# Even mixer of a two-layer decoder trunk: gates and compressed keys ahead of the attention rounds, scores two rounds ahead, exponentials by group; last FFN block and final root rewritten

## The chip, the core and the metric

The kernel runs on one core of a Trainium2 chip. The core has five engines with an instruction queue each: PE (TensorE, matmuls, with a separate queue of weight loads, PEld), DVE (VectorE), ACT (ScalarE), POOL (GpSimd) and SP (SyncE, which here only issues DMAs). Every engine works through its queue in order and waits at semaphores for the others. The metric is device time in microseconds (us) of one execution; times in the profile are us from the start of the span.

## The reference

Two layers, 256 tokens, width 1024. Each layer is `x += 1/2 FFN(norm x); x += mixer(norm x); x += 1/2 FFN(norm x)`, and a last RMSNorm follows. The FFNs are SwiGLU with 2816 hidden columns. The second (odd) layer's mixer, pooling and a diagonal state-space layer, is not touched. The first (even) layer's mixer, which is, computes:

```python
z = h @ w_in                                  # u, v, q, kc, vc, ks, vs, kw, vw, gate logits
# A, gMLP: per head, chunks of 128 tokens
v = (gelu(v) - mean) * rsqrt(var + eps)       # over the 64 columns of a head
s = einsum('hts,bcshd->bcthd', w_s * causal, v) + b
out_a = gelu(u) * s
# B, attention: three branches share q
kc, vc = gelu(blocks(kc) @ w1) @ w2, gelu(blocks(vc) @ w1) @ w2   # compressed keys, 15 blocks
p_c = softmax(q kc * scale)                   # branch 1
o_s = softmax(q ks * scale, causal) @ vs      # branch 2 (all 4 blocks are selected at 256 tokens)
o_w = softmax(q kw * scale, causal) @ vw      # branch 3 (the window of 512 covers all)
out_b = sigmoid(gate) weighted sum of the three
m = concatenate([out_a, out_b]) @ w_out
```

The final norm is `x * rsqrt(mean(x*x) + 1e-6) * g`.

## The kernel before, in words

**Matmuls.** x is kept transposed in SBUF as eight tiles of 128 columns by 256 tokens (`x`, and its split into a high part `xh` and a low part `xl`). Every weight is split too, into `wh` (ACT, a cast, L98) and `wl` (DVE, a subtraction, L108), and each product is the sum of three matmuls: high·high, high·low, low·high (L123 to L125 for products by rows, L134 to L141 for projections, L164 to L166 where tokens are the rows). So the PE does three matmuls of 256 columns where one would stand.

**Weights.** They lie in one stream of units of 128x1024 values, two to a DMA (`raw`, three buffers, issued by SP). `unit` takes the split unit that is due, `used` counts it, and `split_to` then casts and subtracts the next one, up to six units ahead (seven buffers of `wh` and `wl`). With `at["hold"]` set, `used` splits nothing. With `at["wait"]` set, `split_to` casts at once but leaves the DVE subtraction in the list `lows`, from which `chain` takes one after each of two of its ACT steps (`lower(1)`) and `lower()` the rest.

**FFN** (`ffn`). 22 blocks of 128 hidden columns. Block j: two units of gate and up (`proj`, 48 matmuls), `chain(j)` (DVE `e`, ACT `s`, DVE `h`, ACT `hh`, DVE `hl`), then `down(j - 1)` (24 matmuls). After the last block `down(21)` comes directly behind `down(20)`. In all blocks from the fourth on `at["wait"]` is set during `proj`.

**Even mixer** (`even`). The order is written out by hand, since each engine's queue keeps program order. First the projections kk, q0, q1 and v (until 230.5 us in the profile), with rotary embedding on DVE, and `gv`, the gelu of v, on ACT. Then the narrow projection n (values and gate logits, tokens as rows, in banks 2 and 3). Then six rounds of attention: two for the first 128 tokens (four heads a group, width 128, one for each branch) and four for the second (two heads a group, width 256). A round has two groups g. For round i:

- `scores(i)`: PE, into banks 0 and 1, one a group, with the causal mask added by a bf16 matmul; DVE takes the maxima `am` (L555, L556); ACT takes exponentials with the row sums `alr` (L559)
- `norm(i, g)`: DVE multiplies by gate over row sum (L568 to L571)
- `turn(i, g)`: PE transposes four blocks into bank 3 (`pt`, L577), ACT copies them out (`pts`, L579)
- `mix(i)`: PE multiplies by the values `vn`, into banks 6 and 7 (`oT`, L588)

The generator `filling` gives dense matmuls to put between these: compressed keys cc, gate projections u0 and u1, and the first quarter of the output product (`half_out`). The work of branch A and of the compressed keys (`hps`, `kps`, `hid`, `cmp_scores`, `cmp_probs`, `cmp_pv`, `spatial`, `variance`) hangs between the steps of the filling. Round i's scores are written while round i-1 is under way. PSUM has eight banks and each is reused under several names; a name's first write waits for the last reader of the name before. `close` splits `oT` for the output product.

**End.** After the last FFN the sums of squares go through 28 matmuls to `ms` (L228), `rstd` computes the inverse root from an integer guess and three Newton steps on DVE (12 small instructions), 16 transposes turn x into `fo`, and four scaled copies `xo` (two on DVE, two on ACT) go out by four DMAs, two issued by SP and two by ACT.

Of the kernel before, what the change touches and what calls it, by code (L numbers as in the profile page):

```python
# [16 lines left out]
D = 1024  # L17
T = 256
# [18 lines left out]
def even_units():  # L37
    return (pair_units("kk", "q0") + pair_units("q1")
            + [("v", k) for k in range(4)] + [("n", k) for k in range(3)]
            + pair_units("cc") + pair_units("u0") + pair_units("u1")  # L40
            + [("eo", d, k) for d, k in ((0, 0), (0, 1), (1, 0), (1, 1), (0, 2), (1, 2), (0, 3), (1, 3))])
# [16 lines left out]
def trunk(ctx, tc, a, out):  # L58
# [121 lines left out]
    V.memset(ones, 1.0)  # L180
    zero = cst.tile([128, 512], BF, name="zero")
# [35 lines left out]
    def rsqrt(y, v, shape):  # L217
        t = wk.tile(shape, F32, tag=f"rs{shape[1]}", name="rs")
        V.tensor_scalar(y.bitcast(I32), v.bitcast(I32), 1, None, op0=OP.logical_shift_right)
        V.tensor_scalar(y.bitcast(I32), y.bitcast(I32), -1.0, float(0x5F3759DF), op0=OP.mult, op1=OP.add)  # L220
        for _ in range(3):
            V.tensor_tensor(t, y, y, op=OP.mult)
            V.scalar_tensor_tensor(t, t, -0.5, v, op0=OP.mult, op1=OP.mult)
            V.scalar_tensor_tensor(y, t, 1.5, y, op0=OP.add, op1=OP.mult)
# [31 lines left out]
    def ffn(f, after):  # L256
# [41 lines left out]
        for j in range(3, NM):  # L298
# [5 lines left out]
            at["wait"] = True  # L304
# [5 lines left out]
            used()  # L310
        down(NM - 1, after)
        used()

    def even(after):
# [66 lines left out]
        def steps(name, o, halves, done=None):  # L381
            for half in halves:
                for k in range(4):
                    pairs([(name, o)], half, (k,))
                    if k == 3:
                        if half and done:
                            done()
                        used()
                    yield

# [8 lines left out]
        def filling():  # L399
            cps = bank(4, "cps")  # L400
            yield from steps("cc", cps, (0, 1), lambda: widen(cps))
            hps = bank(2, "hps")
            ups = bank(5, "ups")
            for n, _ in enumerate(steps("u0", ups, (0, 1), lambda: ugate(0, ups))):
                for l in (2 * n, 2 * n + 1):
                    P.matmul(hps[:, 0:68], w1[:, l], zcv[:, :, l:l + 529:16], start=l == 0, stop=l == 15)
                if n == 7:
                    V.tensor_copy(hs[0:64], hps[64:128, 1:34])
                    V.tensor_copy(hs[64:128], hps[0:64, 34:67])
                    V.tensor_tensor(hs[0:64], hs[0:64], hps[0:64, 0:33], op=OP.add)  # L410
                    V.tensor_tensor(hs[64:128], hs[64:128], hps[64:128, 35:68], op=OP.add)
                    S.activation(hid[:, :, 0:15], hs[:, 0:32].rearrange("p (g n) -> p g n", g=2)[:, :, 0:15],
                                 AF.Gelu_apprx_tanh, bias=hs[:, 32:33])
                    S.activation(gu[:, 0:2], gu[:, 0:2], AF.Gelu_apprx_tanh)
                    G.tensor_copy(hr[64:128], hid[64:128, :, None, :].to_broadcast([64, 2, 4, 16]))
                yield
            ups1 = bank(5, "ups")
            u1 = steps("u1", ups1, (0, 1), lambda: ugate(1, ups1))

            def dense(g, n=1):  # L420
                for _ in range(n):
                    next(g)
                    yield

            yield from dense(u1, 3)
            kps = bank(2, "kps")
            for g in range(2):
                P.matmul(kps[64 * g:64 * g + 64, 16 * g:16 * g + 16], w2[0:64, :], hid[0:64, g], start=True,
                         stop=True, skip_group_check=True)
            vps2 = bank(4, "vps2")  # L430
            P.matmul(vps2[:, 0:64], hr[64:128].rearrange("p a b c -> p (a b c)"), w2[64:128, :], start=True,
                     stop=True, skip_group_check=True)
            for g in range(2):
                V.tensor_copy(kz[64 * g:64 * g + 64, 16 * g:16 * g + 16], kps[64 * g:64 * g + 64, 16 * g:16 * g + 16])
            V.tensor_tensor(kzs, kz, cse[:, 1], op=OP.mult)
            V.tensor_tensor(kz, kz, cse[:, 0], op=OP.mult)
            V.tensor_tensor(vc.rearrange("p a b c -> p (a b) c"), msel.rearrange("p a b c -> p (a b) c"),
                            vps2[:, None, 0:64].to_broadcast([128, 8, 64]), op=OP.mult)
            yield from dense(u1, 1)
            sp = [spatial(0, 4), spatial(1, 2)]  # L440
            next(sp[0])
            next(sp[0])
            yield
            yield from dense(u1, 1)
            kps = bank(2, "kps2")
            P.matmul(kps[:, 0:32], rot, kzs, start=True, stop=True, skip_group_check=True)
            V.tensor_tensor(kcr, kz, kps[:, 0:32], op=OP.add)
# [1027 lines left out]
```

## Time and profile before

| | |
|---|---|
| three timed runs | 989.79, 990.17 (median), 990.9 us |
| the profiled execution's own time | 990.87 us |
| its span | 989.2 us |
| PE busy | 959.7 us (97%) |
| DVE, ACT, POOL busy | 631.5 (64%), 485.4 (49%), 294.0 us (30%) |
| DMA | 175.47 MB, mean 177 GB/s |

Within the span, the FFN of the first layer runs to 201 us, its mixer to 331.7, the two FFNs that follow to about 717, the odd mixer to about 789, and the last FFN to 977.8. A busy PE is not a PE at full rate: matmul ends are modelled, so the steps from one matmul's start to the next's say more than the busy share. PEclk is the clock that the throttle granted, 1.00 at full rate.

### The profile page before, as it was taken

The page shows a single profiled execution, that of the slowest core. Times are in us where ns is not written, and L with a number is a line of the kernel's source. Part 1 is how long each engine was busy: PE and PEld are TensorE (multiplying, and loading weights), DVE is VectorE, ACT ScalarE, POOL GpSimd, SP SyncE. Part 2 cuts the span into 40 slices and gives each one's busy share as a digit, 9 for nine tenths or more (in the row PEclk, how much of TensorE's full clock was granted, in tenths as well). Part 3 has the DMA queues.
Part 4 walks back from the last instruction along what each step waited for, and adds up shares of the span by engine and source line. Part 5 has one row for each costly group of instructions (what it writes and reads, how often), then busy time and mean ns, then how long its engine had stood idle before and what let it go on. Part 6 is the DMA issues. An engine that isn't in the chain of part 4 may idle for free.

```text
span 989.2 us, 19297 instructions
## 1 busy us (share of the span) xinstructions
PE 959.7 (97%) x8075; PEld 936.7 (95%) x8075; DVE 631.5 (64%) x943; ACT 485.4 (49%) x741; POOL 294.0 (30%) x461
## 2 busy tenths in 40 slices
PE   8999999999878999999999999999999999999997
PEld 6999999998757999999999999999998999999997
DVE  6766655587755775555548754557778676555554
ACT  6544444477544554444445543444465555444442
POOL 1399979010020235554401531438010000000001
PEclk9999999999989999999999999999999999999998
DMA  7655655544312464545443645694553445445431
GB/s 258 244 208 200 227 214 185 207 135 164 129 43 85 164 225 179 197 181 190 180 170 129 233 182 183 208 260 156 211 164 124 180 170 199 187 173 211 171 129 43
DMA packets 32856, 175.47 MB, mean 177 GB/s; under 512 B 7792, under 2 KB 10032, under 8 KB 12928
## 3 DMA queue, kind: packets, MB, share of 16 engines
q1 hardware_dynamic: 29696, 166.21, 46.4%
q0 software_dynamic: 2496, 7.41, 2.8%
q8 instruction: 63, 1.03, 0.4%
q10 hardware_dynamic: 576, 0.62, 0.2%
q14 instruction: 25, 0.20, 0.1%
HBM read 172.12 MB, written 2.10 MB: 176 GB/s over the span
## 4 chain that ended last, share of the span: by engine, by line
PE 87%; DVE 6%; ACT 2%; issue 2%; DMA 1%; POOL 1%; SPq 1%; ACTq 0%; POOLq 0%; DVEq 0%
PE gu L134 16%; PE gu L136 16%; PE gu L141 16%; PE y L125 9%; PE y L124 9%; PE y L123 9%; DVE wl L108 2%; DMA raw<-in_ws 1%; ACT pr L559 1%; DVE pr L571 1%; PE ms L228 0%; PE sc L547 0%; PE glu L125 0%; PE zc L164 0%; PE zd L134 0%
## 5 line engine op out<-in xcount | busy, mean ns | idle before, releaser
L108 DVE TENSOR_TENSOR wl<-raw,wh 128x1024 fp32r<-128x1024 f32 x308 | 382.0, 1252 | 14.9 <-ACT wh L98 14.9
L134 PE MATMUL gu<-xh,wh 128*128 128x256 f32 x1408 | 365.2, 282 | 1.4 <-ACT wh L739 1.1
L136 PE MATMUL gu<-xh,wl 128*128 128x256 f32 x1408 | 364.0, 282 | 0.7 <-DVE wl L740 0.4
L98 ACT CAST wh<-raw 128x1024 fp32r<-128x1024 f32 x308 | 312.0, 1049 | 90.4 <-PE gu L141 41.5
L141 PE MATMUL gu<-xl,wh 128*128 128x256 f32 x1408 | 275.9, 281 | 0.0
L134 PEld LDWEIGHTS gu<-xh,wh 128*128 128x128 f32 x1408 | 265.7, 189 | 3.7 <-ACT wh L739 2.9
L136 PEld LDWEIGHTS gu<-xh,wl 128*128 128x128 f32 x1408 | 264.8, 188 | 2.1 <-DVE wl L740 1.8
L261 DVE TENSOR_TENSOR e<-gu,rb 128x512 f32<-128x512 f32 x88 | 60.8, 690 | 256.9 <-PE gu L141 255.7
L141 PEld LDWEIGHTS gu<-xl,wh 128*128 128x128 f32 x1408 | 213.7, 188 | 0.0
L125 PE MATMUL y<-hl,wh 128*128 128x256 f32 x704 | 198.6, 282 | 1.6 <-DVE hl L272 1.6
L123 PE MATMUL y<-hh,wh 128*128 128x256 f32 x704 | 198.2, 282 | 1.2 <-ACT hh L270 1.2
L124 PE MATMUL y<-hh,wl 128*128 128x256 f32 x704 | 198.3, 282 | 0.0
L264 ACT ACTIVATE s<-e 128x256 f32<-128x256 f32 x88 | 36.8, 418 | 204.4 <-DVE e L261 204.3
L125 PEld LDWEIGHTS y<-hl,wh 128*128 128x128 f32 x704 | 132.5, 188 | 2.4 <-DVE hl L272 2.4
L123 PEld LDWEIGHTS y<-hh,wh 128*128 128x128 f32 x704 | 132.6, 188 | 1.6 <-ACT hh L270 1.4
L124 PEld LDWEIGHTS y<-hh,wl 128*128 128x128 f32 x704 | 132.6, 188 | 0.0
L270 ACT CAST hh<-h 128x256 fp32r<-128x256 f32 x88 | 35.8, 407 | 85.5 <-DVE h L267 85.5
L300 POOL COPY pace<-hl 128x1 f32<-128x1 f32 x25 | 25.0, 1001 | 151.5 <-DVE hl L272 151.5
L206 POOL TENSOR_TENSOR sq<-sq 128x512 f32<-128x512 f32 x10 | 13.7, 1365 | 187.2 <-ACT sq L204 119.0
L761 POOL TENSOR_SCALAR sq<-x,gw 128x256 f32<-128x256 f32 x4 | 3.6, 918 | 184.2 <-DVE x L752 184.2
L789 POOL TENSOR_TENSOR sq<-sq 128x64 f32<-128x64 f32 (+1 forms) x120 | 53.3, 463 | 3.6
L267 DVE TENSOR_TENSOR h<-s,e 128x256 f32<-128x256 f32 x88 | 39.4, 448 | 8.2 <-ACT s L264 8.2
(334 smaller groups left out, 1138.5 us busy)
## 6 DMA issues: line engine op xcount, KB each, us to landing
raw<-in_ws SPq DMA_DIRECT2D x154, 1024.0 KB, 4.8
toep<-kd POOLq DMA_DIRECT2D x8, 256.0 KB, 9.7
raw<-in_ws SPq DMA_DIRECT2D x4, 256.0 KB, 4.4
raw<-in_ws SPq DMA_DIRECT2D x2, 512.0 KB, 8.2
w<-in_w POOLq DMA_DIRECT2D x1, 1024.0 KB, 5.1
bnd<-in_bnd POOLq DMA_DIRECT2D x1, 544.0 KB, 5.5
x<-in_x SPq DMA_DIRECT2D x4, 128.0 KB, 3.6
x<-in_x SPq DMA_DIRECT2D x2, 256.0 KB, 7.5
```

Source lines behind the costliest of these rows:

```text
L98: S.copy(h, src)
L108: V.tensor_tensor(lo, src, h.bitcast(F32), op=OP.subtract)
L123: P.matmul(o, h, ah, start=first, stop=False, skip_group_check=True)
L124: P.matmul(o, lo, ah, start=False, stop=False, skip_group_check=True)
L125: P.matmul(o, h, al, start=False, stop=last, skip_group_check=True)
L134: P.matmul(os, h[:, c], xh[:, 4 * half + k], start=half == 0 and k == 0 and s == 0, stop=False, skip_group_check=True)
L136: P.matmul(os, lo[:, c], xh[:, 4 * half + k], start=False, stop=False, skip_group_check=True)
L141: P.matmul(o[:, T * s:T * s + T], h[:, c], xl[:, 4 * half + k], start=False, stop=half == 1 and k == 3, skip_group_check=True)
L261: V.tensor_tensor(e, gu[j].rearrange("p (a b) -> p a b", a=2), rb[:, None, :].to_broadcast([128, 2, T]), op=OP.mult)
L264: S.activation(s, e[:, 0], AF.Silu)
L267: V.tensor_tensor(h, s, e[:, 1], op=OP.mult)
L789: steps.append(lambda: G.tensor_tensor(o, p, q, op=op))
```

## The change

In the even mixer:

- The weight stream has u0, cc and u1 before n, and the output units in another order.
- `filling` is taken apart. u0, cc and u1 are projected first, without attention between them (`ahead`). `variance` (now with its square on ACT) stands between the halves of cc; `spatial(0)` stands in front of u1's fourth step, the 16 compression matmuls `hps` between its last four.
- All four gelus come before the exponential table is loaded. Then `scores(0)` and its exponentials, then n in three pieces (`narrow`) with `spatial(1)`, `kps` and the rotation of the compressed keys between them. `ah` and `al` get tiles of their own, since n still reads `xh`.
- `scores(i)` no longer does the exponentials; `expo(i, g)` does, per group. Round i now goes: for each group the transposes of round i and, on ACT behind the copy of the transposes, the exponentials of round i+1, then DVE's `norm` of round i+1; after both groups `mix(i)` and `scores(i + 2)`.
- The filling in the rounds is output product alone: three units, 24 steps of three matmuls. One weight unit is split per round.

In `ffn` the last block no longer sets `at["wait"]`, so its two subtractions stand ahead of `chain(21)`. At the end the inverse root is ACT's square root (its table loaded before `down(21)`), a reciprocal and one Newton step, and all four output DMAs are issued by SP.

Three places in the order. The first is PE in u1, and what POOL has there. `sps` are the spatial matmuls, `gv` the normalized v. Before, they stood behind the second mix:

```order
L141 MATMUL ups<-xl,wh 128x256 x2
L588 MATMUL oT<-pts,vn 64x2x128 x4
L480 MATMUL sps<-wst,gv 128x128 x4
L134 MATMUL ups<-xh,wh 128x256
L136 MATMUL ups<-xh,wl 128x256
```

Now they stand in u1's projection, ahead of all attention:

```order
L141 MATMUL ups<-xl,wh 128x256 x2
L406 MATMUL sps<-wst,gv 128x128 x4
L134 MATMUL ups<-xh,wh 128x256
L136 MATMUL ups<-xh,wl 128x256
L134 MATMUL ups<-xh,wh 128x256
L136 MATMUL ups<-xh,wl 128x256
L141 MATMUL ups<-xl,wh 128x256 x2
L590 MATMUL hps<-zcv,w_130 128x68 x4
```

The spatial matmuls moved ahead of six rounds, the variance that they need with them, from inside the first round to cc. On ACT, the same stretch now reads, with one table load after the gelus:

```order
L365 ACT_TABLE_LOAD
L365 ACTIVATE gv<-v_2901,rc 128x8x64
L365 ACTIVATE gv<-v_2902,rc 128x8x64
L98 CAST wh<-raw 128x1024 x2
L575 ACTIVATE sq<-sq 128x512
L98 CAST wh<-raw 128x1024
L556 ACTIVATE sq<-gv 128x1024
L98 CAST wh<-raw 128x1024 x2
L600 ACTIVATE hid<-hs 128x2x15
L602 ACTIVATE sq<-sq 128x512
L604 ACT_TABLE_LOAD
L604 ACTIVATE gate<-ones 128x1
```

The square of gv (L556) now stands behind the gelu of u0 (L575) and a cast. The second place is where the rounds begin, on PE. Before, n was followed by the scores and dense cc:

```order
L166 MATMUL n_3011<-wh,xl 128x280
L547 MATMUL sc<-roped 128x128 x8
L550 LDWEIGHTS identb
L550 MATMUL sc<-negb,identb 128x512
L550 LDWEIGHTS identb
L550 MATMUL sc<-negb,identb 128x512
L134 MATMUL cps<-xh,wh 128x256
```

Now the scores of round 1 stand there, six dense matmuls, and the first transposes:

```order
L473 MATMUL sc<-roped 128x128 x8
L476 LDWEIGHTS identb
L476 MATMUL sc<-negb,identb 128x512
L476 LDWEIGHTS identb
L476 MATMUL sc<-negb,identb 128x512
L123 MATMUL y<-ah,wh 128x256
L124 MATMUL y<-ah,wl 128x256
L125 MATMUL y<-al,wh 128x256
L123 MATMUL y<-ah,wh 128x256
L124 MATMUL y<-ah,wl 128x256
L125 MATMUL y<-al,wh 128x256
L509 MATMUL pt<-ident,pr 128x128 x4
```

DVE has this between the gate's last step and the copy of the values out of bank 3, into which those transposes go:

```order
L643 TENSOR_SCALAR sg<-sg 128x48
L500 RECIPROCAL alr<-alr 128x4
L501 TENSOR_TENSOR alr<-alr,sg 128x4
L503 TENSOR_SCALAR pr<-pr,alr 128x128 x4
...
L480 TENSOR_REDUCE am<-sc 128x4
L481 TENSOR_SCALAR am<-am 128x4
...
L648 TENSOR_SCALAR vn<-n_3277,rc 128x256
L648 TENSOR_SCALAR vn<-n_3278,rc 128x256
```

The lines left out repeat the three of `norm` and the two of the maxima for the second group. The copies `vn`, which before came ahead of the gate and both norms, now come behind them and behind the maxima of round 1. The third place is the end of a first FFN on DVE, before and now:

```order
L261 TENSOR_TENSOR e<-gu,rb 128x512
L108 TENSOR_TENSOR wl<-raw,wh 128x1024
L267 TENSOR_TENSOR h<-s,e 128x256
L108 TENSOR_TENSOR wl<-raw,wh 128x1024
L272 TENSOR_TENSOR hl<-h,hh 128x256
```

```order
L108 TENSOR_TENSOR wl<-raw,wh 128x1024 x3
L266 TENSOR_TENSOR e<-gu,rb 128x512
L272 TENSOR_TENSOR h<-s,e 128x256
L277 TENSOR_TENSOR hl<-h,hh 128x256
```

The two subtractions between the steps of the chain now stand ahead of it. The diff, with the moved bodies cut:

```diff
     return (pair_units("kk", "q0") + pair_units("q1")
-            + [("v", k) for k in range(4)] + [("n", k) for k in range(3)]
-            + pair_units("cc") + pair_units("u0") + pair_units("u1")
+            + [("v", k) for k in range(4)] + pair_units("u0") + pair_units("cc") + pair_units("u1")
+            + [("n", k) for k in range(3)]
...
-            at["wait"] = True
+            at["wait"] = j < NM - 1
...
+        if f == 3:
+            S.activation(gate, ones[:, 0:1], AF.Sqrt)
         down(NM - 1, after)
...
+        ups = bank(5, "ups")
+        ahead("u0", ups)
+        ugate(0, ups)
+        S.activation(gu[:, 0:2], gu[:, 0:2], AF.Gelu_apprx_tanh)
+        cps = bank(7, "cps")
+        pairs([("cc", cps)], 0)
+        used()
+        variance()
+        pairs([("cc", cps)], 1)
+        widen(cps)
+        used()
...
+        def early(n):
+            if n == 3:
+                spatial(0, 5)
+            for l in range(4 * n - 16, 4 * n - 12) if n > 3 else ():
+                P.matmul(hps[:, 0:68], w1[:, l], zcv[:, :, l:l + 529:16], start=l == 0, stop=l == 15)
...
+        ahead("u1", ups1, early)
...
+        S.activation(gate, ones[:, 0:1], AF.Exp)
+        spatial_out(0)
+        scores(0)
+        expo(0, 0)
+        expo(0, 1)
...
+        narrow(2)
+        P.matmul(kps[:, 128:160], rot, kzs, start=True, stop=True, skip_group_check=True)
         for t in range(2):
-            V.tensor_scalar(vn[:, t], nps[t][:, 0:256], rc[:, t:t + 1], None, op0=OP.mult)
             S.activation(sg[:, t], nps[t][:, 256:280], AF.Tanh, scale=hrc[:, t:t + 1])
...
         for g in range(2):
             norm(0, g)
+        scores(1)
+        for t in range(2):
+            V.tensor_scalar(vn[:, t], nps[t][:, 0:256], rc[:, t:t + 1], None, op0=OP.mult)
...
+        go(2)
+        for i in range(6):
+            for g in range(2):
+                turn(i, g)
+                if i < 5:
+                    expo(i + 1, g)
+                    norm(i + 1, g)
+                go(1 if g and i in (2, 3) else 2)
+            if i == 1:
+                cmp_probs()
+            elif i == 2:
+                cmp_transpose()
+            mix(i)
+            if i < 4:
+                scores(i + 2)
+            if i == 0:
+                cmp_scores()
+            elif i == 3:
+                for b in range(2):
+                    cmp_pv(b)
+                close(0)
+            split_to(min(at["used"] + AHEAD, at["split"] + 1))
...
-    rstd(ms)
+    root = wk.tile([128, 2], F32, tag="msv", name="root")
+    S.activation(root, ms[:, 0:2], AF.Sqrt, scale=1.0 / D, bias=eps)
+    mean = wk.tile([128, 2], F32, tag="rs2", name="mean")
+    V.tensor_scalar(mean, ms[:, 0:2], 1.0 / D, 1e-6, op0=OP.mult, op1=OP.add)
+    V.reciprocal(rc, root)
+    newton(rc, mean, wk.tile([128, 2], F32, tag="rs2", name="rs"))
...
-            (nc.scalar if t else nc.sync).dma_start(out[128 * t:128 * t + 128, 512 * h2:512 * h2 + 512], o)
+            nc.sync.dma_start(out[128 * t:128 * t + 128, 512 * h2:512 * h2 + 512], o)
```

More of the change, by code (lines that the diff above doesn't have):

```diff
@@ L379, in even @@
         vc = gm.tile([128, 4, 2, 64], F32, name="vc")
[L381 to L389, printed above, removed]
         def ugate(i, o):
@@ L397, in widen @@
                 V.tensor_tensor(v2(zcv[r, i, 0:512]), v2(o)[r], rb[r, None, :].to_broadcast([64, 2, T]), op=OP.mult)
[L399 to L447, printed above, removed]
-            yield from dense(u1, 1)
-            next(sp[0], None)
-            yield from dense(u1, 1)
-            next(sp[1])
-            yield
-            yield from dense(u1, 1)
-            S.activation(gu[:, 2:4], gu[:, 2:4], AF.Gelu_apprx_tanh)
-            next(sp[1])
-            y[0:2] = [bank(4, "y"), bank(5, "y")]
-            out0 = half_out(0, 0, True, False)
-            yield from dense(out0, 2)
-            next(sp[1], None)
-            yield from cmp_scores()
-            yield from dense(out0, 5)
-            cmp_probs()
-            yield from dense(out0, 1)
-            out1 = half_out(0, 1, False, False)
-            yield from dense(out1, 2)
-            cmp_transpose()
-            yield
-            for b in range(2):
-                cmp_pv(b)
-                yield
-            yield from dense(out1, 6)
@@ L473, in even @@
-        ah, al = xh[:, 0:4], xl[:, 0:4]
+        ah = gm.tile([128, 4, T], F32R, name="ah")
+        al = gm.tile([128, 4, T], F32R, name="al")
+        gated = {}
         def spatial(i, b):
@@ L507, in cmp_scores @@
                              stop=t == 1 and j == 3, skip_group_check=True)
-                if not t:
-                    yield
             V.tensor_tensor(pc, sc[:, 0:256].rearrange("p (t h n) -> p t h n", t=2, h=8),
@@ L629, in variance, with ahead, narrow @@
             G.memset(kz, 0.0)
-        fill = filling()
-        def go(n):
-            for _ in range(n):
-                next(fill, None)
+        def ahead(name, o, before=None):
+            for half in range(2):
+                for k in range(4):
+                    if before:
+                        before(4 * half + k)
+                    pairs([(name, o)], half, (k,))
+                used()
[9 more added lines that the diff above has]
+        widen(cps)
+        used()
+        hps = bank(4, "hps")
+        ups1 = bank(6, "ups")
+        def early(n):
[3 more added lines that the diff above has]
+                P.matmul(hps[:, 0:68], w1[:, l], zcv[:, :, l:l + 529:16], start=l == 0, stop=l == 15)
+            if n == 7:
+                at["hold"] = True
+        ahead("u1", ups1, early)
+        V.tensor_copy(hs[0:64], hps[64:128, 1:34])
+        V.tensor_copy(hs[64:128], hps[0:64, 34:67])
+        V.tensor_tensor(hs[0:64], hs[0:64], hps[0:64, 0:33], op=OP.add)
+        V.tensor_tensor(hs[64:128], hs[64:128], hps[64:128, 35:68], op=OP.add)
+        ugate(1, ups1)
+        S.activation(hid[:, :, 0:15], hs[:, 0:32].rearrange("p (g n) -> p g n", g=2)[:, :, 0:15],
+                     AF.Gelu_apprx_tanh, bias=hs[:, 32:33])
+        S.activation(gu[:, 2:4], gu[:, 2:4], AF.Gelu_apprx_tanh)
+        G.tensor_copy(hr[64:128], hid[64:128, :, None, :].to_broadcast([64, 2, 4, 16]))
+        S.activation(gate, ones[:, 0:1], AF.Exp)
[3 more added lines that the diff above has]
+        expo(0, 1)
+        V.tensor_scalar(hrc, rc, 0.5, None, op0=OP.mult)
         nps = [bank(2, "n0"), bank(3, "n1")]
-        at["hold"] = True
-        for n in range(3):
+        kps = bank(6, "kps")
+        def narrow(n):
             h, lo = unit(("n", n))
```

99 lines of the change are left out of this document (54 added, 45 removed).

## The prediction

> **What bounds the kernel now.** I read the page's busy shares first, then the waits of PE over the whole span, then the stretches of the even mixer by granted clock, then PE's timeline at the waits.
>
> ```profile
> PE 959.7 (97%) x8075; PEld 936.7 (95%) x8075; DVE 631.5 (64%) x943; ACT 485.4 (49%) x741; POOL 294.0 (30%) x461
> ```
>
> PE is busy nearly throughout, so a gain can only come from PE's idle time, from a low clock, or from the two ends. Who PE waits for (us in total, times, longest):
>
> ```profile
> PE pt L577 <- ACT pts L579: 8.3, 4, 3.8
> PE sps L480 <- DVE vc L437: 4.0, 1, 4.0
> PE pctp L529 <- POOL pc L524: 1.9, 1, 1.9
> PE y L125 <- DVE hl L272: 1.6, 3, 0.5
> ...
> PE kps L428 <- ACT hid L412: 1.3, 1, 1.3
> ...
> PE oT L534 <- ACT pct L530: 0.5, 1, 0.5
> ```
>
> All but the fourth row lie in the even mixer: 8.3 + 4.0 + 1.9 + 1.3 + 0.5 = 16.0 us of idle PE. The fourth is the end of three FFNs. Then the clock (PEclk) and three places of PE's timeline, where the bracket is the idle time before:
>
> ```profile
> 240.00:250.00 10.00, 7.18 (x53) 6.36 (x54) 8.13 (x21) 9.24 (x23) 0.00 (x0) 0.88 0.14 40
> 300.00:310.00 10.00, 7.68 (x55) 5.55 (x53) 4.98 (x14) 3.45 (x9) 1.47 (x1) 1.00 0.30 107
> ```
>
> ```profile
> 247.76 1.12 PE L577 MATMUL pt<-ident,pr 128*128 128x128 f32 x4 [2.74 <-ACT pts L579]
> 274.67 1.81 PE L480 MATMUL sps<-wst,gv 128*128 128x128 f32 x8 [3.95 <-DVE vc L437]
> 282.77 1.06 PE L480 MATMUL sps<-wst,gv 128*128 128x128 f32 x8
> 312.99 0.66 PE L577 MATMUL pt<-ident,pr 128*128 128x128 f32 x4 [1.06 <-ACT pts L579]
> ```
>
> After an idle time of 2.74 or 3.95 us the same work is slower: transposes 1.12 against 0.66 us, spatial matmuls 1.81 against 1.06. The 1.9 us wait for `pc` (it ends at 302.9) leaves the clock at 1.00. Three waits are long enough (2.74, 3.95 and the 3.8 of the first waits row). The slow time after one is about 3.5 us, in which half the work is done, so each costs some 1.7 us, 2.5 after the longest; I put the three at 5.8. So the mixer holds 16.0 + 5.8 = 21.8 us that a better order could at most win back. The question is how much of it returns as new waits.
>
> **The new PE order, first wait.** The stretch that changes runs between these two starts, and the row between them gives the length of a unit:
>
> ```profile
> 230.48 0.29 PE L164 MATMUL n<-wh,xh 128*128 128x280 f32 x1
> 317.43 0.39 PE L123 MATMUL y<-xh,wh 128*128 128x256 f32 x1
> 331.72 0.28 PE L134 MATMUL gu<-xh,wh 128*128 128x256 f32 x1
> ```
>
> From 317.43 to 331.72 PE does five units of 24 matmuls without a wait: 14.29 / 5 = 2.86 us a unit. From 230.48 it now does u0 (two units, 5.7), cc (5.7) and three of u1's eight steps (2.1), and at 244.0 it reaches the spatial matmuls. They need `gv`, centred and scaled. That chain crosses four engines:
>
> ```profile
> 233.13 0.18 DVE L362 TENSOR_SCALAR mu<-mu 128x16 f32<-128x16 f32 x1
> 245.17 1.11 ACT L659 ACTIVATE sq<-gv 128x1024 f32<-128x1024 f32 x1
> 255.99 1.22 DVE L624 TENSOR_REDUCE var<-sq 128x16 f32<-128x1024 f32 x1
> 259.86 1.91 POOL L627 TENSOR_TENSOR gv<-gv,rstd 128x1024 f32<-128x1024 f32 x1 [24.50 <-DVE alr L568]
> 263.50 0.68 DVE L392 TENSOR_TENSOR sq<-ups,rb 128x512 f32<-128x512 f32 x1
> 285.69 1.05 ACT L98 CAST wh<-raw 128x1024 fp32r<-128x1024 f32 x1
> 292.04 0.62 POOL L514 TENSOR_TENSOR pc<-pc,cm 128x256 f32<-128x256 f32 x1
> 301.16 1.22 DVE L108 TENSOR_TENSOR wl<-raw,wh 128x1024 fp32r<-128x1024 f32 x1
> 301.39 1.47 POOL L524 TENSOR_TENSOR pc<-pc,cl 128x256 f32<-128x256 f32 x1 [8.72 <-DVE cl L523]
> ```
>
> The last three rows show POOL and DVE excluding each other: a POOL product that takes 0.62 us alone took 1.47 when it came 0.23 us after a DVE subtraction of 1.22. So: `mu` is done at 233.3; DVE starts a `wl` (to 234.5); POOL's centring, which nothing hindered before, waits for it and takes 1.91 (to 236.4); DVE's next `wl` waits for that (to 237.6); then u0's scaling (238.3), on ACT its gelu (0.6), a cast (1.05) and the square (about 1.0, to 241.0); DVE, with a `wl` until 241.2, needs from the reduction's start to POOL's 259.86 - 255.99 = 3.9 us (245.0); POOL scales (1.91, to 246.9). PE waits 246.9 - 244.0 = **2.9 us**. Without the exclusion it is 1.3 less (wl, gelu and square start when u0 is done, at 236.2), and this is the lower end; a cast or two more in the way is the upper, 4.5. An idle time of 2.9 lies above the 2.74 that was followed by a low clock: plus 1.6.
>
> What is queued behind on PE is all of the mixer, so nothing covers this wait.
>
> **Second wait.** The first transposes of round 0 go into bank 3, which `vn` must have emptied. DVE does that behind the gate, two norms and the maxima of round 1.
>
> ```profile
> 236.74 1.16 PE L547 MATMUL sc<-roped 64*128 64x128 f32 x16
> 238.09 0.47 PE L134 MATMUL cps<-xh,wh 128*128 128x256 f32 x1
> 239.93 0.87 DVE L652 TENSOR_SCALAR vn<-n,rc 128x256 f32<-128x256 f32 x2
> 242.01 0.49 ACT L653 ACTIVATE sg<-n,hrc 128x24 f32<-128x24 f32 x2
> 245.04 4.62 DVE L108 TENSOR_TENSOR wl<-raw,wh 128x1024 fp32r<-128x1024 f32 x4
> 252.25 0.69 DVE L555 TENSOR_REDUCE am<-sc 128x4 f32<-128x512 f32 x1
> 253.77 0.17 DVE L556 TENSOR_SCALAR am<-am 128x4 f32<-128x4 f32 x1
> ```
>
> From the last matmul of n: the gate and both norms 245.04 - 242.01 = 3.0 us, the maxima 253.9 - 252.25 = 1.7, `vn` 0.9, hand-overs 0.1: 5.7. In that time PE has the rotation (0.3), the scores of round 1 (238.09 - 236.74 = 1.35) and six dense matmuls (0.7, with the change of shape 0.9): 2.55. PE waits **3.1 us**, and 1.7 for the clock. Bounds: 2.5 (maxima overlapped as well as possible, by 0.6) to 3.9 (POOL's last product of branch A, near 1.3 us, in the way of `sg`, by 0.8).
>
> **The rounds.** Four table loads of ACT (after the first gelu of a group and back) leave the mixer's middle, and with them the waits that they feed. ACT's work in a round of the second half is now:
>
> ```profile
> 281.63 0.59 ACT L579 COPY pts<-pt 128x512 f32<-128x512 f32 x1 [0.80 <-PE pt L577]
> 283.87 0.47 ACT L559 ACTIVATE pr<-sc,am 128x256 f32<-128x256 f32 x1 [1.65 <-PE sps L480]
> ```
>
> Two copies (1.2), the exponentials of both groups (283.87 to 285.69, 1.8) and one cast (1.05): 4.1 us. The second copy stands behind the first group's exponentials (0.9), while PE has 0.7 of dense work between the two sets of transposes and 0.4 to 0.7 behind; so each `mix` waits a little. With scores two rounds ahead no round waits for maxima. I take 0.4 us a round, six rounds, 2.5 us: between nothing and the 1.06 that such a wait still cost late in the old order (row 312.99), which is 6.4. These waits are too short for the clock.
>
> **Weights.** PE asks for no unit sooner: DMA chunk, cast and subtraction still run up to six units ahead, and in the rounds, where PE uses half a unit a round, one is split per round. SP's queue holds nothing else there. Zero, and if that cover failed one cast and subtraction, 2.3 us.
>
> **Sum of the mixer.** Removed 21.8; new 2.9 + 1.6 + 3.1 + 1.7 + 2.5 = 11.8; fewer changes of shape (`hps` cuts the dense work four times, no longer eight), 0.5. Gain 21.8 - 11.8 + 0.5 = **10.5 us**.
>
> The Trainium skill (TensorE: Matmul & The Clock Gate, "Part 1: The HAM clock gate") says that the array's clock falls to half after an idle window of about 3.4 us, windows that run free of the kernel. By it both new waits, being shorter, could pass without a low clock; this trace differs, with 2.74 us followed by slow transposes.
>
> **FFN ends.** The fourth row of the waits, 1.6 us, is a chain whose last step comes late:
>
> ```profile
> 518.76 1.22 DVE L108 TENSOR_TENSOR wl<-raw,wh 128x1024 fp32r<-128x1024 f32 x1
> 520.23 1.22 DVE L108 TENSOR_TENSOR wl<-raw,wh 128x1024 fp32r<-128x1024 f32 x1
> ```
>
> They stand between `e`, `h` and `hl`. Ahead of the chain they run while PE does the block's last 2.86 us, and `hl` comes 1.6 us sooner where 0.5 was missing. Gain **1.6 us**; if the second `wl` is late by its cast, 0.5 remains of it.
>
> **Tail.**
>
> ```profile
> 980.87 0.16 DVE L233 TENSOR_SCALAR msv<-ms 128x2 f32<-128x2 f32 x1 [0.89 <-PE ms L228]
> 983.04 0.16 DVE L224 SCALAR_TENSOR_TENSOR rc<-rs,rc 128x2 f32<-128x2 f32 x1
> 980.69 2.86 PE L1306 MATMUL fo<-ident,sq 128*128 128x128 f32 x16
> 985.17 0.35 ACTq L1323 DMA_DIRECT2D out<-xo  x1
> ```
>
> The 12 small steps (980.87 to 983.2) become a root, a reciprocal and three: 1.1 us. But the transposes end at 983.55, and the last copy (0.7) can only start then: 984.3, against 985.17 when ACT, having issued a DMA between its copies, issued the last. SP then issues it. Gain **0.85 us**, between 0.4 (SP has the four issues one after another) and 1.2.
>
> Total 10.5 + 1.6 + 0.85 = 12.95. The profiled execution took 990.87 us (span 989.2), which gives 977.9; the median is 0.7 lower: 990.17 - 12.95 = **977.2 us**.
>
> **Rivals.**
> - *The two waits cost no clock, or the first hardly occurs.* The low clock follows an idle time that is near the shortest seen to do it (2.74). Without it 3.3 us return: 973.9. With the first wait at its lower end too, 972.3. Against it: 2.9 and 3.1 lie above 2.74. Chance 0.2. It is here that the skill's rule would put the result.
> - *The rounds are paced by ACT and DVE after all.* If every round waits 1.06 us and the round with the compressed scores runs into a 2.7 us wait of its own, the rounds cost 6.4 + 2.7 + 1.7 = 10.8 instead of 2.5: 985.5. For it: DVE has about 4.8 us of norms, maxima and `wl` in a round against ACT's 4.1, and all take turns. Chance 0.14.
> - *Nothing is won*: the waits move one for one, within 2 us of 990.2. For it: PE's order is rigid, and the first wait shows how early work can outrun its inputs. Against it: the four longest waits all hang on table loads or maxima that are now taken ahead. Chance 0.04.
> - *Slower: the clock stays low through the rounds.* If each round holds a PE wait of 2.7 us or more, every round runs at half clock. Its dense and small matmuls, about 4.5 us at full clock (28 in six rounds), double: 977.2 + 28 + 6 x 2.3 = 1019. It decides from three such rounds on (half of 42 is 21, more than the gain of 13). Against it: scores are two rounds ahead. Chance 0.04.
>
> **How the numbers follow.** My forecast (both new waits with a slow clock after them, short waits in the rounds) has 0.58, with its own range 974.5 to 981. The range to hold 8 of 10 reaches to the first rival's lower value and into the second: 970.5 to 983.5. A measurement of this kernel tells about 0.2% (2 us) from no change. Faster 0.58 + 0.2 + 0.14 = 0.92, same 0.04, slower 0.04.
>
> **What would show it.** In the new profile: the four gelus with one table load before and one after; PE waiting for POOL's `gv` at `sps` near 244 for about 3 us, and for DVE's `vn` at the first `pt` for about 3, each followed by some 3.5 us at half clock; no wait above 1 us in the rounds; the next FFN's first `gu` near 321 instead of 331.72; no PE wait for `hl`. It would be wrong if PE's waits in the mixer sum to under 5 or over 14 us, or if the mixer's end and the total do not move together.

## The result and the profile after

The kernel before took 990.53 us (median of four runs, 989.79 to 991.72), the changed one 973.42 (four runs, 971.23 to 974.56): a ratio of 0.9819, 95% interval 0.9808 to 0.9831, or 17.1 us less. That is inside the range, and 3.8 us less than the 977.2 that was forecast. The profiled execution is the lowest of the four, 971.23 us with a span of 969.5, so against the profiled execution before (990.87) it shows 19.6.

The page's busy shares:

```profile
span 969.5 us, 19281 instructions
...
PE 953.1 (98%) x8075; PEld 932.8 (96%) x8075; DVE 632.3 (65%) x937; ACT 481.5 (50%) x740; POOL 295.7 (31%) x461
```

The engines have nearly the same to do: PE does the same 8075 matmuls, in 6.6 us less busy time (959.7 before), and ACT works 3.9 us less. Who PE waits for (us in total, times, longest), the two largest rows:

```profile
PE pt L509 <- DVE vn L648: 3.0, 1, 3.0
PE sps L406 <- POOL hid L561: 2.4, 1, 2.4
```

Of the mixer's waits before, five rows and 16.0 us, none is left. These two, 5.4 us, are the two new waits of the prediction; the other rows above 1 us (1.4, 1.3 and 1.2) lie in the first FFN. The row `y L125 <- hl` at the end of the FFNs is gone. PE's timeline at the two places, and at the first five of the six groups of products with the values (`oT`), the bracket being idle time before:

```profile
244.84 1.16 PE L406 MATMUL sps<-wst,gv 128*128 128x128 f32 x8 [2.39 <-POOL hid L561]
246.55 1.11 PE L590 MATMUL hps<-zcv,w 128*128 128x68 f32 x8
...
268.28 0.63 PE L509 MATMUL pt<-ident,pr 128*128 128x128 f32 x4 [3.01 <-DVE vn L648]
...
270.88 1.66 PE L520 MATMUL oT<-pts,vn 128*64 128x256 f32 x8
...
278.47 1.18 PE L520 MATMUL oT<-pts,vn 128*64 128x256 f32 x8
...
283.37 1.62 PE L520 MATMUL oT<-pts,vn 128*64 128x256 f32 x8
...
288.49 1.53 PE L520 MATMUL oT<-pts,vn 128*64 128x256 f32 x8
...
295.67 1.19 PE L520 MATMUL oT<-pts,vn 128*64 128x256 f32 x8
```

Three things are to be seen. The waits come at 244.84 and 268.28, for `gv` (POOL's product ends at 244.79, and the memset of `hid` is what POOL does next) and for `vn`. The work behind them is *not* slow: the transposes take 0.63, not the 1.12 that followed 2.74 us of idle time before. And the rounds are not quite free of waits, though no bracket says so: eight such products took 1.08 us in the timeline of before,

```profile
256.20 1.08 PE L588 MATMUL oT<-pts,vn 128*64 128x256 f32 x8
```

and take 1.66, 1.18, 1.62, 1.53 and 1.19 here, 1.8 us more in all. A row of the weight queue in the timeline of after names the cause:

```profile
271.46 0.62 PEld L520 LDWEIGHTS oT<-pts,vn 128*64 128x64 f32 x6 [0.39 <-ACT pts L511]
```

The first two weights load at once, the other six wait for the second copy, which stands behind the first group's exponentials. The third group, at 283.37, has the same row with 0.35. The granted clock of after in the two stretches with a long wait:

```profile
240.00:250.00 10.00, 7.61 (x65) 7.41 (x65) 8.33 (x21) 1.05 (x1) 4.18 (x4) 1.00 0.28 107
260.00:270.00 10.00, 6.99 (x63) 6.33 (x61) 7.12 (x25) 2.24 (x7) 2.59 (x2) 1.00 0.00 0
```

It is 1.00 in both (the third number from the right). Before, the stretch from 240 to 250 had 0.88 and the next 0.95, behind the first long wait, and behind the other two:

```profile
270.00:280.00 10.00, 6.05 (x40) 5.51 (x36) 6.13 (x19) 3.31 (x11) 1.28 (x1) 0.83 0.29 105
290.00:300.00 10.00, 6.36 (x32) 4.87 (x34) 3.84 (x13) 5.24 (x14) 1.94 (x3) 0.66 0.00 0
```

By stage, the 19.7 us between the two spans are found with the sums of squares `ms` that begin and end a block. Of before, then of after, from the chain of waits:

```profile
208.60 0.34 PE ms L228 x4
338.99 0.34 PE ms L228 x4
...
977.81 3.03 PE ms L228 x28
```

```profile
206.78 0.49 PE ms L233 x4
322.11 0.34 PE ms L233 x4
...
959.23 3.02 PE ms L233 x28
```

The even mixer took 130.39 us and takes 115.33: **15.1 us**. The tail behind the last `ms` took 11.4 (977.81 to 989.2) and takes 10.3 (959.23 to 969.5): **1.1**. The start came 1.8 earlier (208.60 to 206.78), of which 1.0 stands ahead of the first `y`, where a weight DMA landed that much sooner (at 12.95, before at 13.94); no edit of the change bears on it. The rest, 1.7, is in the blocks between (638.82 and 637.12 from the mixer's end to the last `ms`).

### The profile page after: what moved, and what is told of

Same layout as the page of the kernel before. It is cut to its first block, busy times and chain, and to the rows that moved or that the text cites. A ratio compares the mean times of both kernels' runs of the same rounds, so it can differ in the third digit from the quotient of the medians.

```text
span 969.5 us, 19281 instructions
## 1 busy us (share of the span) xinstructions
PE 953.1 (98%) x8075; PEld 932.8 (96%) x8075; DVE 632.3 (65%) x937; ACT 481.5 (50%) x740; POOL 295.7 (31%) x461
## 4 chain that ended last, share of the span: by engine, by line
PE 93%; DVE 3%; ACT 1%; DMA 1%; issue 1%; SPq 1%; POOL 0%; ACTq 0%; POOLq 0%
PE gu L134 17%; PE gu L136 17%; PE gu L141 17%; PE y L125 10%; PE y L123 10%; PE y L124 10%; PE oT L520 1%; DVE wl L108 1%; PE pt L509 1%; DMA raw<-in_ws 1%; PE sc L473 1%; PE ms L233 1%; PE zd L134 0%; PE zc L164 0%; PE glu L125 0%
## 5 line engine op out<-in xcount | busy, mean ns | idle before, releaser
L125 PE MATMUL y<-hl,wh 128*128 128x256 f32 x704 | 198.4, 282 | 0.0
L125 PEld LDWEIGHTS y<-hl,wh 128*128 128x128 f32 x704 | 132.6, 188 | 0.2 <-DVE hl L277 0.2
L272 DVE TENSOR_TENSOR h<-s,e 128x256 f32<-128x256 f32 x88 | 39.2, 446 | 10.3 <-ACT s L269 10.3
```

The lines of the kernel that those rows point to most:

```text
L125: P.matmul(o, h, al, start=False, stop=last, skip_group_check=True)
L272: V.tensor_tensor(h, s, e[:, 1], op=OP.mult)
```

## Experiments

**The changed kernel again, and its parts alone.** Four kernels beside the same runs of the kernel before, 991.21 us in that set: the changed kernel unaltered; the new mixer with the FFN ends and the tail as before; and the kernel before with one edit each.

```diff
-            at["wait"] = True
+            at["wait"] = j < NM - 1          (last FFN block alone)

-    rstd(ms)                                 (tail alone)
+    S.activation(root, ms[:, 0:2], AF.Sqrt, scale=1.0 / D, bias=eps)
+    ...
+    V.reciprocal(rc, root)
+    newton(rc, mean, ...)
...
-            (nc.scalar if t else nc.sync).dma_start(...)
+            nc.sync.dma_start(...)
```

> The changed kernel once more, for the spread of its times. Theory 1 (clock): the two PE waits of 2.4 and 3.0 us lie at the border of what lowers the clock, so executions differ by which of the two lowered it: times spread over 3 us, and each time falls with its mean granted clock, about 1.7 us a lowered stretch (970 us x 0.0009 of mean clock each). Theory 2 (the spread has another cause, the DMA at the start or the weights): times differ as much, but not with the clock.

> The new even mixer alone, with the FFN ends and the tail as before. Theory 1: 973.4 + 1.6 (FFN ends) + 0.85 (tail) = 975.9, 14.6 less than before. Rival: FFN ends and tail bring more than these rows say (the profiles differ by 19.7 us, the mixer in them by 15.1), then 977 to 978.

> The kernel before with only the last FFN block's subtractions ahead of its chain. Theory 1: three PE waits of 0.53 us go, 1.6 us less. Rival: the next stall stands behind it (the third subtraction in front of the residual), 0 to 0.5.

> The kernel before with only the new tail (root by table, DMAs by SP). Theory 1: 0.85 us less, the last copy starting at the end of the transposes. Rival: no gain or a loss, since ACT now does the root in front of its copies and SP issues four DMAs one after another: 0 to 0.4 us less.

| kernel | us (lowest to highest) | ratio, 95% interval | gain |
|---|---|---|---|
| changed kernel again | 973.12 (972.34 to 974.78) | 0.9819, 0.9805 to 0.9833 | 18.1 |
| mixer alone | 977.42 (976.26 to 978.32) | 0.9862, 0.9847 to 0.9878 | 13.8 |
| FFN ends alone | 989.47 (987.62 to 991.16) | 0.9984, 0.9975 to 0.9993 | 1.7 |
| tail alone | 989.42 (988.04 to 991.26) | 0.9982, 0.9972 to 0.9991 | 1.8 |

The parts add up: 13.8 + 1.7 + 1.8 = 17.3 beside 18.1. The FFN ends are as forecast; the tail is more than its 0.85, but its interval (0.9 to 2.8) all but holds that, and the trace's 1.1 does not differ from it by much. The mixer is where the forecast was short, 13.8 against 10.5. With 977.42 us the mixer alone lies at its rival: ends and tail bring more than their rows said. The eight executions of the changed kernel sort by their mean clock, as theory 1 of the first text expected: 971.2 to 972.5 us at 0.997, 972.9 and 973.9 at 0.995, 973.8 to 974.8 at 0.993.

The profile of the mixer alone has the same two waits, of 2.38 and 3.0 us, and this time slow work behind the first (PE's timeline):

```profile
245.46 1.16 PE L402 MATMUL sps<-wst,gv 128*128 128x128 f32 x8 [2.38 <-POOL hid L557]
247.37 1.81 PE L586 MATMUL hps<-zcv,w 128*128 128x68 f32 x8
```

The changed kernel, profiled again, has it behind the second:

```profile
268.62 1.09 PE L509 MATMUL pt<-ident,pr 128*128 128x128 f32 x4 [3.01 <-DVE vn L648]
270.79 1.05 PE L509 MATMUL pt<-ident,pr 128*128 128x128 f32 x4
272.57 1.08 PE L520 MATMUL oT<-pts,vn 128*64 128x256 f32 x8
```

So the same wait, to 0.01 us, is followed by full speed in one execution and by a low clock in another. Over the profiled runs of this study that hold these waits (the first 2.4 us, the second 3.0; the clock read in the stretches around them):

| profiled kernel | behind 2.4 us | behind 3.0 us | mixer, `ms` to `ms` |
|---|---|---|---|
| changed | full | full | 115.33 |
| changed, again | full | low | 116.10 |
| mixer alone | low | low | 117.17 |
| `vn` early (below) | low | wait gone | 114.57 |
| spatial late (below) | wait gone | low | 114.01 |
| scores one round ahead (below) | full | low | 123.57 |
| table loads (below) | full | full | 129.23 |

A low clock came behind 2 of 6 first waits and 4 of 6 second ones. It cost 0.8 us (116.10 - 115.33) for one and 1.8 for both, half of the 1.6 and 1.7 of the prediction. A reason can be read in the last fence: behind the slow transposes the eight products take 1.08 again, not 1.66, since the copy that they waited for has had time to finish. A part of what the clock costs is taken out of a wait that would have come anyway.

**TensorE kept busy in both waits.** If the scatter of the changed kernel's times comes from the clock, it should go when PE isn't idle.

```diff
+        def keep(b, n):
+            w_ = bank(b, "warm")
+            for _ in range(n):
+                P.matmul(w_, zero[:, 0:128], zero, start=True, stop=True)
...
             if n == 3:
+                keep(0, 10)
                 spatial(0, 5)
...
         go(2)
+        keep(6, 12)
         for i in range(6):
```

> The changed kernel with dummy bf16 matmuls of 512 columns on PE in the two waits (10 before the first spatial matmuls, 12 before the first transposes), into banks that are free: PE does not idle there, the waits themselves stay. Theory 1 (clock): the clock never falls in the mixer, so the times close up near the fastest of the kernel without them, 971 to 971.5, and the mean clock near 0.997 to 0.998. Theory 2: the spread and the median of the changed kernel stay as they are (971.2 to 974.6, median 973.4), or get worse by the time of the dummies.

Measured: 971.51 us, 971.37 to 971.74 (ratio 0.9798, 0.9784 to 0.9811). The lowest time is that of the changed kernel; what has gone is the upper part, and four runs lie within 0.4 us, where eight of the changed kernel cover 3.6. PE's timeline shows the wait filled and full speed behind it, and its mixer takes 115.33 us (206.88 to 322.21), as long as the changed kernel's without a low clock:

```profile
265.21 2.76 PE L575 MATMUL warm<-zero 128*128 128x512 bf16 x11
268.37 0.63 PE L509 MATMUL pt<-ident,pr 128*128 128x128 f32 x4 [0.40 <-DVE vn L654]
```

So the chance of a low clock behind the two waits costs the median some 1.6 to 1.9 us (973.12 and 973.42, less 971.51; 2.1 by the ratios). The two low clocks of the profiled runs (1.8 us together) don't reach all of the 3.6; what the rest is stays open.

**The two waits taken away.** Each by order alone: `vn` is read from its bank ahead of the gate, the norms and the maxima; the square and the variance go to other places, and the spatial matmuls to the end of `u1`.

```diff
(vn early)
+        for t in range(2):
+            V.tensor_scalar(vn[:, t], nps[t][:, 0:256], rc[:, t:t + 1], None, op0=OP.mult)
         ...
-        for t in range(2):
-            V.tensor_scalar(vn[:, t], nps[t][:, 0:256], rc[:, t:t + 1], None, op0=OP.mult)

(spatial late)
         def variance():
-            S.activation(gsq, gv..., AF.Square)
...
         pairs([("cc", cps)], 0)
         used()
-        variance()
+        S.activation(gsq, gv..., AF.Square)
         pairs([("cc", cps)], 1)
         widen(cps)
+        variance()
...
-            if n == 3:
+            if n == 7:
                 spatial(0, 5)
```

> The changed kernel with the two copies vn directly behind the rotation of the compressed keys, ahead of the gate, the norms and the maxima. Theory 1: the first transposes wait for the first norm alone; the wait of 3.0 us falls below 0.5, less 1.7 where the clock fell there: 969 to 971. Rival (the wait only moves): the transposes or the copies behind them then wait for the maxima of round 1, and less than 1 us is won.

> The changed kernel with the compressed keys' widening ahead of the variance on DVE and the first spatial matmuls ahead of the last step of u1 instead of its fourth. Theory 1: gv is ready by then (about 247.3 against 248), the wait of 2.4 us goes, less 1.7 where the clock fell there: 969 to 971. Rival (the wait only moves): PE waits at hps for the widened keys or at the spatial matmuls as before, and less than 1 us is won.

> Both of these. Theory 1: no PE wait above 1 us is left in the mixer and the clock stays up: 973.4 - 2.4 - 3.0 less the lowered clock of about 2, 966 to 967.5, and little spread. Rival: the gains overlap, 969 or more.

| kernel | us (lowest to highest) | ratio, 95% interval |
|---|---|---|
| `vn` early | 970.59 (969.36 to 970.62) | 0.9785, 0.9771 to 0.9799 |
| spatial late | 970.53 (969.87 to 970.75) | 0.9787, 0.9773 to 0.98 |
| both | 967.51 (967.38 to 968.01) | 0.9759, 0.9746 to 0.9773 |

Both together gain 5.8 us on the median of the changed kernel's eight runs (973.36), and each run beats all of these. PE's waits of that version, and its timeline at the two places:

```profile
PE oT L520 <- ACT pts L511: 0.8, 1, 0.8
...
PE sps L406 <- POOL hid L560: 0.3, 1, 0.3
```

```profile
248.92 1.16 PE L406 MATMUL sps<-wst,gv 128*128 128x128 f32 x8 [0.35 <-POOL hid L560]
...
263.52 0.60 PE L509 MATMUL pt<-ident,pr 128*128 128x128 f32 x4
```

The waits fall by 2.1 (2.4 to 0.3) and by 2.2 (3.0 to the 0.8 that `oT` now waits), 4.3 in all, and the low clock can't follow: 4.3 + 1.6 = 5.9. In the trace the mixer takes 110.95 us (207.23 to 318.18), 4.4 less than the 115.33 without a low clock, which is the waits. The two new waits were a matter of order, and the change would have won more with them mended.

**What the rounds owe to the scores.** The scores of round i+1 go back to where the kernel before had them, one round ahead. The edit does one thing more: both transposes and their copies now come ahead of the exponentials of both groups.

```diff
         for i in range(6):
+            turn(i, 0)
+            go(1)
+            turn(i, 1)
+            if 0 < i < 5:
+                scores(i + 1)
+            go(1)
             for g in range(2):
-                turn(i, g)
...
-            if i < 4:
-                scores(i + 2)
```

> The changed kernel with scores one round ahead again, as in the kernel before: the scores of round i+1 are written between the two sets of transposes of round i, just ahead of that round's exponentials, everything else as changed. If the rounds are free of waits because the maxima are a round older than the exponentials (my theory), PE now waits 1 to 2 us a round on the chain from maxima to exponentials to norm, and the time goes up by 5 to 8 us to 978 to 981. The rival, that the dense work between covers this chain anyway and that the gain came from the table loads alone, has it within 1 us of 973.3, with no wait of PE above 0.5 us in the rounds.

Measured: 978.47 us (976.43 to 980.09; ratio 0.9872, 0.9854 to 0.989), 5.3 more than the changed kernel's 973.1. PE's waits:

```profile
PE pt L509 <- ACT pts L511: 2.6, 5, 0.8
PE pt L509 <- DVE pr L503: 2.5, 3, 0.9
```

That is 5.1 us in eight short waits, for the norms of DVE and the copies of ACT: the theory's chain. The dense work does not cover it. That 5.1 and 5.3 are so close is chance, though. The second copy no longer stands behind exponentials, so the products take 1.08 us again at full clock and some 1.8 us of hidden waits are gone. And in the profiled execution, the slowest of the four, the mixer is 8.2 us longer (123.57 - 115.33), since the clock fell twice: behind the wait of 3.0 us that the changed kernel has too, and once where no wait was longer than 0.94 us (scores of 1.13 us take 2.08):

```profile
290.23 0.63 PE L509 MATMUL pt<-ident,pr 128*128 128x128 f32 x4 [0.94 <-DVE pr L503]
...
292.59 2.08 PE L473 MATMUL sc<-roped 64*128 64x256 f32 x8
```

So the place of the scores costs about 3.3 us by its waits (5.1 - 1.8, an estimate); that the clock is the rest is not shown by itself.

**What they owe to the table loads.**

```diff
             for g in range(2):
                 turn(i, g)
+                if 0 < i < 5 and not g:
+                    S.activation(gate, ones[:, 0:1], AF.Gelu_apprx_tanh)
```

> The changed kernel with a one-column gelu on ACT ahead of the first group's exponentials in rounds 1 to 4, so that ACT loads two tables more in each of these rounds; its result isn't used. If the table loads fed the old waits, ACT's 4.1 us of work in a round grows by two loads of about 1.3 us, more than the round has, and PE waits for the copies: plus 6 to 10 us, 979 to 983. The rival, that ACT has this time free because the dense work and the second set of transposes cover it, has it within 1 us of 973.3.

Measured: 988.94 us (984.62 to 991.4; ratio 0.9976, 0.9961 to 0.9991), 15.8 more than the changed kernel's 973.1. Eight table loads thus take back almost the whole gain, and more than the theory gave. They are twice the four that the change took out of the rounds, so 15.8 is not the price of those four. ACT's timeline in one round, then PE's waits:

```profile
284.70 0.59 ACT L511 COPY pts<-pt 128x512 f32<-128x512 f32 x1 [0.89 <-PE pt L509]
285.30 1.28 ACT L667 ACT_TABLE_LOAD   x1
286.60 0.20 ACT L667 ACTIVATE gate<-ones 128x1 f32<-128x1 f32 x1
286.82 1.28 ACT L491 ACT_TABLE_LOAD   x1
288.11 0.47 ACT L491 ACTIVATE pr<-sc,am 128x256 f32<-128x256 f32 x1
...
289.03 0.58 ACT L511 COPY pts<-pt 128x512 f32<-128x512 f32 x1
```

```profile
PE oT L520 <- ACT pts L511: 9.8, 4, 2.6
```

Each round waits 2.4 to 2.6 us, nearly the 2.8 of two loads and the small gelu. The theory set ACT's 4.1 us of work against a round, 5.0 and 5.3 us long in the timeline of after, and let about 1 us of it be slack. But the second copy stands in ACT's queue behind whatever comes ahead of the first group's exponentials, and PE's products need that copy: between the two there is hardly any slack, as the 1.66 of the rows of after shows. The count of an engine's work says how long it *can* take; the place in its queue decides here. Behind two of these four waits the clock also fell:

```profile
290.00:300.00 10.00, 7.44 (x43) 0.83 0.29 105
300.00:310.00 10.00, 7.63 (x46) 0.91 0.01 2
310.00:320.00 10.00, 10.00 (x75) 0.92 0.50 165
```

(Start and length of the stretch, PE busy, clock, DMA share and rate.) In the profiled execution, 985.26 us, the mixer is 13.9 us longer than in that of the changed kernel (129.23 - 115.33), 9.8 of it idle time and some 3.4 the low clock of these three rows.

**The low clock of the kernel before, by itself.** The prediction put it at 5.8 us behind three waits. Fillers in these waits leave the order alone.

```diff
+            if i in (0, 3):
+                keep(0, 16 if i else 11)
             turn(i, 1)
...
             sp = [spatial(0, 4), spatial(1, 2)]
+            w_ = bank(3, "warm")
+            for _ in range(17):
+                P.matmul(w_, zero[:, 0:128], zero, start=True, stop=True)
             next(sp[0])
```

> The kernel before, with 11, 17 and 16 matmuls of zeros (bfloat16, 512 columns, about 0.21 us each) in its three long waits, of 2.74, 3.95 and 3.78 us; their result isn't used, and the work and its order are as before. The waits stay, only TensorE isn't idle in them. The prediction put the low clock behind these three waits at 5.8 us: 985.2 beside 991, with the clock near 1.00 in all stretches of the mixer. If the slow work behind them has another cause than the idle time (first touches of operands after a wait, say), it stays at 991 within 1 us, with transposes of 1.12 us as before.

> The kernel before with fillers again, sized by the trace of the first try: 10 instead of 17 at the spatial matmuls, where 17 outlasted the wait by 1.2 us, and 5 and 9 more ahead of the compressed keys' weights (a wait of 1.3 us) and of the compressed probabilities' transposes (2.7 us), each followed by slow work in that trace. If a clock that stays up is worth its 5.8 us by itself, the time is 984 to 986. The rival, that the kernel before is paced in its rounds by ACT, DVE and POOL, so that PE made faster waits longer, has it at 988 to 990 with the clock near 1.00 in all stretches.

The second kernel has 10 in place of 17, and 5 ahead of the first `kps` and 9 ahead of `cmp_transpose` more. Measured: 990.13 us for the first (ratio 0.9987, 0.9977 to 0.9998, beside 990.38) and 990.81 for the second (0.9991, 0.9981 to 1.0, beside 990.98). Neither shows 5.8 us, though the mean clock of both rose from 0.989 to 0.995. The slow work did come from the idle time: behind the filled waits the transposes take 0.66 us, no longer 1.12. But in the first kernel the clock fell in other places, at 269.4 behind a wait of 1.31 us (which the kernel before passes at full clock) and at 303.5 behind one of 2.72. The second's timeline says how little this settles:

```profile
254.16 1.08 PE L593 MATMUL oT<-pts,vn 128*64 128x256 f32 x8
...
267.87 1.24 PE L641 MATMUL warm<-zero 128*128 128x512 bf16 x4 [2.31 <-ACT pts L584]
...
276.83 1.05 PE L485 MATMUL sps<-wst,gv 128*128 128x128 f32 x8
...
295.06 0.66 PE L582 MATMUL pt<-ident,pr 128*128 128x128 f32 x4 [0.33 <-ACT pts L584]
```

The fillers at 267.87 used a bank that ACT had not yet emptied, and themselves waited 2.31 us, where `kps` had waited 1.3; behind that the clock was at half from 269.2 to 276.0. Counted piece by piece: from the mixer's first `ms` to the first products 47.6 us before (208.60 to 256.20) and 46.6 in both kernels with fillers, so the first low clock was worth 1.0, not 1.7. From the spatial matmuls to the mixer's last `ms` 64.3 before (274.67 to 338.99) and 62.1 in the second kernel (276.83 to 338.90), and that piece holds the low clocks of both later waits: together they were worth about 2.2, where the prediction has 4.1 (5.8 - 1.7). One reason stands in the timelines: with PE at full speed the next transposes wait 1.61 us for ACT's copy, not 0.69. The middle piece grew, from 18.5 to 22.7, by the fillers' own doing, and ate both. What the clock would be worth there was not measured.

## Why the prediction came out as it did

The mechanism held: PE's idle time in the middle of the mixer was the price, and taking the table loads and the maxima out of the rounds removed it. The tests in reverse show both at work, though not their shares: scores one round ahead cost 5.3 us, part of it by the clock, and twice the loads cost 15.8. The forecast (two new waits and short ones in the rounds) is right in kind. That the median, 973.4, lies at the number of its first rival (973.9, the waits without the low clock) is luck: the low clock still costs it 1.6 to 1.9, and without it, with fillers, the time is 971.5. The waits and the rounds cost less than forecast. By terms:

- **Waits removed, 16.0 us**: all five rows are gone, as predicted.
- **First wait, 2.9 us**: at the place and on the chain foretold, 2.4. The exclusion of POOL and DVE that lengthened the chain is there: in the timeline of after, POOL's centring, 1.91 us before, takes 2.78 behind a `wl`, and two `wl` of 1.22 take 4.07 with it:

```profile
231.56 4.07 DVE L108 TENSOR_TENSOR wl<-raw,wh 128x1024 fp32r<-128x1024 f32 x2
231.77 2.78 POOL L370 TENSOR_TENSOR gv<-gv,mu 128x1024 f32<-128x1024 f32 x1 [27.36 <-DVE mu L369]
```

- **Second wait, 3.1 us**: 3.0.
- **Low clock behind them, 3.3 us: the step that failed.** None in the first profiled execution, 0.8 in the second, 1.8 with the mixer alone, and by fillers 1.6 to 1.9 in the median. Two errors are in it. "2.9 and 3.1 lie above 2.74" took one observation for a threshold, while a wait of one length falls on either side. And the price was counted as slow work alone, though a slow PE also shortens its next wait. The prediction cited the Trainium skill (TensorE: Matmul & The Clock Gate, "Part 1: The HAM clock gate") with idle windows of some 3.4 us that run free of the kernel. Free windows of that length agree with these traces, where the clock changes only at steps of 3.41 us (last section) and 3.01 us was followed once by 0.63 and once by 1.09. Read as a need for 3.4 us of idle time, as the prediction reads it, the rule does not agree: a wait of 2.38 us was enough here, and once 1.31.
- **Rounds, 2.5 us**: 1.8, on the mixes and for the cause named, the second copy. They show on the weight queue, not on PE.
- **Low clock removed, 5.8 us, and shapes, 0.5**: with the terms above the profiled mixer gives 15.1 + 2.4 + 3.0 + 1.8 - 16.0 = 6.3 for the two, which is their sum. It is a remainder, though: the pieces that could be measured came to 1.0 and 2.2 where 1.7 and 4.1 stood. The two need not contradict each other, since fillers leave the old waits standing, which grow when PE is faster, and the change removes waits and slow work together; but this is argued, not shown. The prediction also put the dearest low clock behind the longest wait: behind 3.95 us it lasted 3.4 us, behind 3.78 it lasted 6.8.
- **FFN ends, 1.6**: 1.7 by themselves. **Tail, 0.85**: 1.1 in the trace, 1.8 (0.9 to 2.8) timed. SP's four issues, feared as a loss, hold up the last one by 0.2 us: its copy ends at 965.4 in the timeline of after, and the last of the four issues starts at 965.6:

```profile
964.29 1.81 SPq L1332 DMA_DIRECT2D out<-xo  x4
964.71 0.69 ACT L1329 ACTIVATE xo<-fo,rc 128x512 f32<-128x512 f32 x1 [0.51 <-PE fo L1310]
```

In the mixer 10.5 were forecast and the profiled execution won 15.1: 3.3 for the clock, 0.7 in the rounds and 0.6 in the two waits make up the difference. The rival of rounds paced by ACT and DVE needed waits of 1 us a round, and is what the kernel with table loads became. The sign by which the prediction would have been wrong, under 5 or over 14 us of PE's waits in the mixer, was not met: 5.4, or 7.2 with the rounds. One slip is in the rivals: with the first wait at its lower end, 1.3 us less, 973.9 becomes 972.6, not 972.3.

## What to carry to other kernels

Read an engine's slack from what stands ahead of the one instruction that another engine needs, not from the sum of its work in a round: eight table loads of 1.28 us cost 15.8 us although the sum left 1 us a round. After a large reordering look at the first waits it leaves behind: here two of them were mended by order alone for another 5.8 us, a third of the whole gain. And price a low clock behind waits of 1 to 4 us as a chance, with less than the slow work as its cost, since the next wait shrinks; some matmuls of zeros in the wait take the chance away, if their bank is free.

## What was not expected of the hardware

A low clock came at fixed steps. Read in stretches of 0.1 us, the granted clock of the kernel before is 0.50 from 247.7 to 251.1, from 275.0 to 278.4 and from 292.1 to 298.9: all six changes lie multiples of 3.41 us apart (1, 8, 9, 13 and 15 from the first), and the same holds within each profiled execution whose mixer has a low clock. So it lasts 3.4 or 6.8 us, and it can begin 1.4 us after PE has started again (246.9 behind the wait that ends at 245.46, mixer alone). Counted over these steps in eleven profiled executions: each of the 20 steps with 1.9 us or more of idle PE was followed by one at half clock, of 11 at full clock with 1.45 to 1.83 us two were, of those with less none. A wait is thus harmless when an edge of the steps divides it; that this is what happened in the executions without a low clock is inferred, since their steps can't be seen.

Accordingly, idle times of TensorE of equal length (2.39 and 2.38 us, 3.01 and 3.01 us) were followed by full speed in some executions and by a low clock in others, 2 of 6 and 4 of 6 times. The low clock cost less than the slow work behind it, 0.8 us for one and 1.8 for two, as the next wait shrank. And a wait can be hidden from the list of PE's waits when it falls inside a group of matmuls: there the weight queue has it, and the group's row is longer (1.66 against 1.08 us).
